# Where 1 / rms and the norm weight enter the two FFNs of a Hymba layer

## The chip, the cores and the metric

The kernel runs on one core of a Trainium2 chip. The time is the device time of one execution in microseconds; several executions give a median. The engines are TensorE (PE; PEld is its weight load), VectorE (DVE), ScalarE (ACT), GpSimd (POOL) and SyncE (SP), which issues most transfers.

## The reference, cut to what matters

One layer for a prompt of 1024 tokens with 16 meta tokens in front, and 8 sample tokens: T = 1048 tokens, D = 1024, D_FF = 2816, all fp32.

```python
def rmsnorm(x, w):
    y = xf * lax.rsqrt(jnp.mean(xf * xf, axis=-1, keepdims=True) + EPS)
    return (y * w.astype(jnp.float32)).astype(x.dtype)

def swiglu(x, wg, wu, wd):
    return (jax.nn.silu(x @ wg) * (x @ wu)) @ wd

# h += 0.5 * swiglu_1(rmsnorm(h));  h += mixers(rmsnorm(h)) @ w_out
# h += 0.5 * swiglu_2(rmsnorm(h));  final rmsnorm
```

The change concerns only `rmsnorm(h) @ wg` and `rmsnorm(h) @ wu`. Since 1 / rms is one factor per token and the norm weight one factor per input row, `rmsnorm(h) @ W = (1 / rms) * (h @ (w * W))`.

## The kernel before, in words

Activations are held transposed, features on the 128 partitions and tokens along the free axis. The tokens fall into two halves (c = 0, 1) of two quarters each, Q = 262 tokens a quarter. A product of fp32 accuracy is made of three matmuls (`mm3`, lines L143, L144 and L145): each operand is split into a high part (a ScalarE cast) and a low part (a VectorE subtraction). For weights these are L137 and L138, for activation operands L272 and L277.

**Gate and up by seven products.** FFN1 and FFN2 have 22 pairs each. A `pair` makes one block of 128 columns of gate and up for all tokens. Gate and up (two columns), the two halves of D (two rows) and the two quarters of a token half form a 2 x 2 by 2 x 2 block product, done with seven products instead of eight, in the order `ORDER = (1, 6, 2, 5, 7, 3, 4)`. Each product is done for both token halves, so a pair has 14 steps of 12 matmuls of 128x262. The left factors are sums of the four loaded weight tiles (gate and up, upper and lower rows; loads L354 numbered 1, 7, 4, 2; sums 5, 6, 7, 3 at L359), made anew for each pair. The right factors are sums of operand blocks (`Blocks`, sums L260), made once for each FFN and used by all 22 pairs.

**After a product** `post` works on it. Products 2, 3 and 4 accumulate in the banks of 1, 5 and 7:

| product | what post does |
|---|---|
| 1 | z: copy of the bank (ACT, L444) |
| 6 | v = bank + z (DVE, L446) |
| 2 | g0 = silu(bank) (ACT, L448) |
| 5 | x = bank + v (DVE, L450) |
| 7 | u1 = bank + x (DVE, L452) |
| 3 | g1 = silu(bank + v) (DVE L454, ACT L455) |
| 4 | u0 = bank + v (DVE, L457), then the hidden rows g * u (DVE, L462 twice) |

An accumulating product can start only when the post of the bank's first product has read it: 2 after z, 3 after x, 4 after u1.

**What sets the order.** Each FFN runs under a schedule written by hand (`manual_schedule` for PE, DVE, ACT and SP): a list of steps, and functions hung before a step with `S.before`. For a pair that begins at step s0, `LEADS` puts the four weight loads before steps s0 - 10, -10, -9, -9, the sums before -7, -7, -6, -5, and the seven splits before s0 - 4 + 2i. An engine works its queue in order. The hidden rows and differences of them (L534) are stored to DRAM by SP (L537) for the down projection, and the loads of the next pair's weights stand behind such stores in SP's queue.

**Operands before the change.** For FFN1, `Input` loads x in nine tiles of 128 tokens, squares them (L837), transposes them on PE, copies them to feature-major form, forms 1 / rms, spreads it over the partitions by a matmul with ones (L881), and multiplies it and the norm weight into the operand blocks (L890, 32 operations of 128x262). For FFN2, `Norm` sums the squares of h while `out_proj` still runs (L201, L202, `nf2.end`), forms 1 / rms (L159 to L163), and `Blocks.scaled` multiplies it and the norm weight into the blocks (L253, 32 operations). The first half's blocks are made in the second half of `out_proj`, the second half's after `out_proj`.

**Pools.** Operand blocks come from 30 `u` slots of T elements, hidden rows from 8 `s` slots, raw weights from 8, split weights from 6; PSUM has two 2-bank `acc` tiles and four `mis` banks.

Of the kernel before, what the change touches and what calls it, by code (L numbers as in the profile page):

```python
# [17 lines left out]
P = 128  # L18
# [163 lines left out]
class Norm:  # L182


    def __init__(self, K, h):
        self.K, self.h = K, h
        self.rt = {}
        self.sq = {}

    def r(self, q):  # L190
        return self.rt[q // 2][:, (q % 2) * Q : (q % 2) * Q + Q]
# [12 lines left out]
    def end(self, q, table=True):  # L204
        K = self.K
        if q // 2 not in self.rt:
            self.rt[q // 2] = K.t(2 * Q)
        ps = K.psm()
        K.nc.tensor.matmul(ps[:, :Q], K.ones[D], self.sq[q], start=True, stop=True)
        K.rstd(self.r(q), ps[:, :Q], Q, self.an if table else None)  # L210

# [29 lines left out]
class Blocks:  # L241


    def __init__(self, K, half):
        self.K, self.half = K, half
        self.b, self.op = {}, {}

    def scaled(self, norm, wcol):
        for p, k0, n in ((1, 0, 0), (7, 0, 1), (2, 4, 0), (3, 4, 1)):
            q = 2 * self.half + n  # L250
            self.b[p] = self.K.slot("u", T)
            for k in range(4):
                self.K.nc.vector.scalar_tensor_tensor(self.b[p][:, k * Q : k * Q + Q], norm.h[k0 + k][:, q * Q : q * Q + Q], wcol[:, k0 + k : k0 + k + 1], norm.r(q), ALU.mult, ALU.mult)  # L253

    def sum_(self, p):
        K, b = self.K, self.b
        x, y = {5: (7, 1), 6: (3, 5), 7: (3, 7), 4: (2, 6)}[p]
        if p not in b:
            b[p] = K.slot("u", T)
        K.nc.vector.tensor_sub(b[p], b[x], b[y])  # L260

    def sums(self):
        for p in (5, 6, 7, 4):
            self.sum_(p)

    def steps(self):


        def cast(*ps):
            for p in ps:  # L270
                self.op[p] = self.K.slot("u", T, F32R), self.K.slot("u", T, F32R)
                self.K.nc.scalar.copy(self.op[p][0], self.b[p])  # L272

        def low(*ps):
            for p in ps:
                hi, lo = self.op[p]
                self.K.nc.vector.tensor_sub(lo, self.b[p], hi.bitcast(F32))  # L277

        def begin():
            cast(1, 2)  # L280
            low(1)
            self.sum_(5)
            self.sum_(6)
            cast(6, 5)

        def more():
            low(5)
            self.sum_(7)
            cast(7, 3)

        def last():
            self.sum_(4)
            cast(4)
            low(7)

        return [begin, lambda: low(6), lambda: low(2), more, last, lambda: low(3, 4)]

    def split(self, p):
        K = self.K
        self.op[p] = K.slot("u", T, F32R), K.slot("u", T, F32R)  # L300
        K.split(self.b[p], *self.op[p])
# [44 lines left out]
def left(K, S, s0, srcs, n, at):  # L346


    nc = K.nc
    raw, w = {}, {}  # L350

    def load(p, src):
        raw[p] = K.raw(n * P)
        nc.sync.dma_start(raw[p].rearrange("p (k c) -> p k c", k=n), src)  # L354

    def sum_(p, x, y, op):
        if p not in raw:
            raw[p] = K.raw(n * P)
        nc.vector.tensor_tensor(raw[p], raw[x], raw[y], op)  # L359

    def split(p):
        w[p] = K.split_w(raw[p])

    loads = [lambda p=p, src=src: load(p, src) for p, src in zip((1, 7, 4, 2), srcs)]
    sums = [
        lambda: sum_(5, 7, 4, ALU.add),
        lambda: sum_(6, 5, 1, ALU.subtract),
        lambda: sum_(7, 1, 7, ALU.subtract),
        lambda: sum_(3, 2, 6, ALU.subtract),
    ]  # L370
    splits = [lambda p=p: split(p) for p in ORDER]
    if at:
        for fns, ds in zip((loads, sums, splits), at):
            for fn, d in zip(fns, ds):
                S.before(s0 + d, fn)
        return w
    return w, loads, sums, splits


LEADS = (-10, -10, -9, -9), (-7, -7, -6, -5), [2 * i - 4 for i in range(7)]  # L380
# [45 lines left out]
def pair(K, S, wg, wu, f, ops, hid, first=None):  # L426
# [8 lines left out]
    srcs = [wg[:, 0:4, fs], wu[:, 0:4, fs], wu[:, 4:8, fs], wg[:, 4:8, fs]]  # L435

    def temp(n, cs):
        if n not in tm:
            tm[n] = halves(K.t(2 * Q))
        return tm[n][:, cs]  # L440

    def post(p, cs, b):
# [4 lines left out]
        elif p == 2:  # L447
            nc.scalar.activation(temp("g0", cs), b, AF.Silu)  # L448
        elif p == 5:
            nc.vector.tensor_add(temp("x", cs), b, temp("v", cs))  # L450
        elif p == 7:
            nc.vector.tensor_add(temp("u1", cs), b, temp("x", cs))  # L452
        elif p == 3:
            nc.vector.tensor_add(temp("g1", cs), b, temp("v", cs))  # L454
            nc.scalar.activation(temp("g1", cs), temp("g1", cs), AF.Silu)  # L455
        else:
            nc.vector.tensor_add(temp("u0", cs), b, temp("v", cs))  # L457
            if "h" not in tm:
# [5 lines left out]
    if not first:  # L464
        w = left(K, S, s0, srcs, 4, LEADS if f > 1 else (*LEADS[:2], [2 * i - 3 for i in range(7)]))
        Unit(K, w, [o.op for o in ops], 4, post).both(S)
        return
    w, loads, sums, splits = left(K, S, s0, srcs, 4, None)
    order, blocks, between = first
    steps = [o.steps() for o in ops]  # L470
    if order == "w":
        between(loads, sums)
        blocks(0)
        splits[0]()
        for i, fn in enumerate(steps[0][:3]):
            fn()
            if i == 0:
                blocks(2)
            if i < 2:
                splits[i + 1]()  # L480
        for i, fn in enumerate(steps[0][3:]):
            S.before(s0 + 1 + i, fn)
            S.before(s0 + 1 + i, splits[3 + i])
        S.before(s0 + 1, lambda: blocks(3))
    else:
        for fn in loads:
            fn()
        blocks(0)
        for fn in steps[0] + sums + splits[:6]:
            fn()  # L490
        S.before(s0 + 6, between)
    S.before(s0 + 4, lambda: blocks(1))
    for i, fn in zip((4, 5, 5, 6, 7, 8), steps[1]):
        S.before(s0 + i, fn)
    S.before(s0 + 9, splits[6])
    unit = Unit(K, w, [o.op for o in ops], 4, post)
    for ps_ in (ORDER[:6], ORDER[6:]):
# [179 lines left out]
def ffn(K, wg, wu, wd, ops, src, first, after):  # L677
# [9 lines left out]
    with K.tc.manual_schedule(engines={E.PE, E.DVE, E.Activation, E.SP}):  # L687
        S = Steps()
        hidden = Hidden(K)
        for i in range(NF // 2):  # L690
            hid, e = [], []
            for f in (2 * i, 2 * i + 1):
                hid.append([])
                pair(K, S, wgv, wuv, f, ops, hid[-1], first if f == 0 else None)
# [98 lines left out]
def token_rows(i, meta, prompt, sample):  # L793

    if i == 0:
        return [(0, NM, meta), (NM, P - NM, prompt[0 : P - NM, :])] if meta is not None else [(NM, P - NM, prompt[0 : P - NM, :])]
    t0 = P * i - NM
# [5 lines left out]
class Input:  # L803
# [3 lines left out]
    def __init__(self, K, a, wcol, ops):  # L807
        self.K, self.wcol, self.ops = K, wcol, ops
        self.a = a
        self.b, self.x, self.n, self.r = {}, {}, {}, {}  # L810
        self.st = K.sml.tile([P, 3, 9], F32, tag="st0", name="st0", bufs=1)
# [874 lines left out]
```

## Time and profile before

| what | value |
|---|---|
| three runs | 2152.72, 2160.46, 2165.0 us; median 2160.46 |
| profiled execution | 2155.25 us, span 2153.5 us, mean granted clock 0.971 |
| busy share of the span | PE 94%, DVE 65%, ACT 36%, POOL 6% |
| FFN1: first product's matmul | 34.07 us |
| FFN1: second pair; end of the last pair | 87.20 us; about 517 us |
| FFN2: first product's matmul; second pair | 1412.49 us; 1456.1 us |
| FFN2: end of the last pair | about 1886 us |

A pair of steady state takes 20.46 us, and TensorE has no gap in it: 14 steps of 12 matmuls, 0.1218 us apart. A duration in a row of the trace is that of one operation; two operations of ScalarE or VectorE in a row overlap by some 0.1 us, so their starts lie closer than their durations (a cast of 128x512 lasts 0.61 us, and the next one starts after 0.51).

### The profile page before, as it was taken

To read this page: it belongs to the slowest core of one execution; us is meant where nothing else is said; L and a number is where in the kernel's file an instruction comes from. 1 tells how busy PE (TensorE), PEld (TensorE's weight loads), DVE (VectorE), ACT (ScalarE), POOL (GpSimd) and SP (SyncE) were. 2 spreads that over 40 slices of the span, in tenths; PEclk is the share of its full clock that TensorE was granted. 3 is DMA by queue.
4 is the path that set the end of the run, shared out by engine and by line. 5 is a ranking of instruction groups with operands and counts; after the bars stand their busy time and mean duration, and the time that the engine had idled before them with its cause. 6 is when DMAs were issued, how large, how long until landed. Compare 5 with 4: busy or idle time off the path is not lost.

```text
span 2153.5 us, 38152 instructions
## 1 busy us (share of the span) xinstructions
PE 2013.7 (94%) x15502; PEld 1960.3 (91%) x15502; DVE 1407.0 (65%) x2380; ACT 774.7 (36%) x1406; POOL 138.1 (6%) x175
## 2 busy tenths in 40 slices
PE   5799999999899899799999998969999999989996
PEld 4799999999899889688989987959999999989996
DVE  5766666666787675596365456776666666668863
ACT  5322222223334543572432335442222222324441
POOL 1000000000002110321011001210000000000000
PEclk6899999999999999899999999989999999999998
DMA  6142332337956511452022043213233242587741
GB/s 201 30 120 84 96 112 82 104 99 218 310 182 195 157 49 31 118 154 74 32 73 77 25 152 125 88 55 105 75 120 97 83 119 85 174 264 228 213 149 58
DMA packets 325031, 259.16 MB, mean 120 GB/s; under 512 B 17712, under 2 KB 301104, under 8 KB 324848
## 3 DMA queue, kind: packets, MB, share of 16 engines
q1 hardware_dynamic: 324040, 254.58, 39.3%
q8 instruction: 122, 2.00, 0.4%
q10 hardware_dynamic: 592, 2.10, 0.3%
q14 instruction: 53, 0.43, 0.1%
q0 software_dynamic: 224, 0.04, 0.0%
HBM read 191.26 MB, written 65.47 MB: 119 GB/s over the span
## 4 chain that ended last, share of the span: by engine, by line
PE 79%; DVE 10%; DMA 4%; ACT 3%; issue 2%; POOL 1%; SPq 0%; DVEq 0%; ACTq 0%; POOLq 0%
PE acc L143 24%; PE acc L144 24%; PE acc L145 24%; PE mis L1336 1%; DMA r<-in_w_ffn_down_dram 1%; DVE u L277 1%; DVE s L633 1%; DVE u L260 1%; DMA s<-in_x_prompt_dram 1%; DMA u<-hd 1%; DVE ws L138 1%; DVE s L1350 1%; DVE ws L615 1%; DVE s L1338 0%; PE mis L1375 0%
## 5 line engine op out<-in xcount | busy, mean ns | idle before, releaser
L143 PE MATMUL acc<-u,ws 128*128 128x262 f32 (+2 forms) x4504 | 1324.2, 295 | 72.1 <-DVE s L633 21.5
L144 PE MATMUL acc<-u,ws 128*128 128x262 f32 (+2 forms) x4504 | 1316.0, 292 | 6.2 <-DVE u L277 5.0
L145 PE MATMUL acc<-u,ws 128*128 128x262 f32 (+2 forms) x4504 | 1313.1, 292 | 0.1
L143 PEld LDWEIGHTS acc<-u,ws 128*128 128x128 f32 x4504 | 856.9, 190 | 90.6 <-issue 27.7
L144 PEld LDWEIGHTS acc<-u,ws 128*128 128x128 f32 x4504 | 860.6, 191 | 8.8 <-DVE u L277 5.9
L145 PEld LDWEIGHTS acc<-u,ws 128*128 128x128 f32 x4504 | 856.8, 190 | 0.9 <-DVE ws L615 0.6
L138 DVE TENSOR_TENSOR ws<-r,ws 128x512 fp32r<-128x512 f32 x396 | 272.7, 692 | 231.0 <-ACT ws L137 231.0
L137 ACT CAST ws<-r 128x512 fp32r<-128x512 f32 x396 | 227.0, 617 | 77.4 <-PE acc L145 58.2
L455 ACT ACTIVATE t<-t 128x524 f32<-128x524 f32 (+1 forms) x46 | 28.7, 623 | 314.3 <-DVE t L454 314.3
L359 DVE TENSOR_TENSOR r<-r,r 128x512 f32<-128x512 f32 x176 | 118.6, 693 | 13.4 <-DMA r<-in_w_ffn_up_dram 11.8
L202 POOL TENSOR_TENSOR t<-t,t 128x262 f32<-128x262 f32 x56 | 53.1, 964 | 815.9 <-ACT t L201 815.9
L633 DVE SCALAR_TENSOR_TENSOR s<-acc,s 128x524 f32<-128x524 f32 (+1 forms) x120 | 77.4, 661 | 41.5 <-PE acc L145 40.5
L562 DVE TENSOR_TENSOR u<-u,u 128x1048 fp32r<-128x1048 f32 (+1 forms) x84 | 96.9, 1158 | 8.4 <-ACT u L558 8.4
L448 ACT ACTIVATE t<-acc 128x524 f32<-128x524 f32 (+1 forms) x46 | 27.1, 589 | 182.2 <-PE acc L145 182.2
L610 ACT CAST ws<-r 128x512 fp32r<-128x512 f32 (+1 forms) x84 | 48.0, 582 | 104.1 <-DMA r<-in_w_ffn_down_dram 45.9
L558 ACT CAST u<-u 128x1048 fp32r<-128x1048 f32 (+1 forms) x84 | 83.2, 993 | 1.4 <-DMA u<-hd 1.4
L615 DVE TENSOR_TENSOR ws<-r,ws 128x512 fp32r<-128x512 f32 (+1 forms) x84 | 56.9, 690 | 40.5 <-ACT ws L610 40.5
L610 ACT CAST ws<-u 128x512 fp32r<-128x512 f32 (+1 forms) x72 | 42.1, 584 | 113.5 <-DVE u L605 110.0
L444 ACT COPY t<-acc 128x524 f32<-128x524 f32 (+1 forms) x46 | 26.5, 577 | 146.6 <-PE acc L145 146.6
L454 DVE TENSOR_TENSOR t<-acc,t 128x524 f32<-128x524 f32 (+1 forms) x46 | 31.2, 679 | 58.8 <-PE acc L145 58.8
L615 DVE TENSOR_TENSOR ws<-u,ws 128x512 fp32r<-128x512 f32 (+1 forms) x72 | 47.2, 656 | 28.4 <-ACT ws L610 28.4
L462 DVE TENSOR_TENSOR s<-t,t 128x524 f32<-128x524 f32 (+1 forms) x92 | 58.5, 677 | 1.6
(353 smaller groups left out, 1764.1 us busy)
## 6 DMA issues: line engine op xcount, KB each, us to landing
hd<-s SPq DMA_DIRECT2D x170, 262.0 KB
r<-in_w_ffn_down_dram SPq DMA_DIRECT2D x128, 256.0 KB
u<-hd SPq DMA_DIRECT2D x56, 524.0 KB
r<-in_w_ffn_gate_dram SPq DMA_DIRECT2D x88, 256.0 KB
r<-in_w_ffn_up_dram SPq DMA_DIRECT2D x88, 256.0 KB
r<-in_w_in_dram SPq DMA_DIRECT2D x56, 256.0 KB
r<-in_w_ffn_down_dram SPq DMA_DIRECT2D x64, 192.0 KB
u<-hd SPq DMA_DIRECT2D x28, 393.0 KB
```

Source lines behind the costliest of these rows:

```text
L137: self.nc.scalar.copy(hi, src)
L138: self.nc.vector.tensor_sub(lo, src, hi.bitcast(F32))
L143: mm(ps, whi, xhi, start=first, stop=False, skip_group_check=more)
L144: mm(ps, whi, xlo, start=False, stop=False, skip_group_check=more)
L145: mm(ps, wlo, xhi, start=False, stop=last, skip_group_check=more)
L359: nc.vector.tensor_tensor(raw[p], raw[x], raw[y], op)
L462: nc.vector.tensor_mul(halves(hid[0][:, n * 2 * Q : n * 2 * Q + 2 * Q])[:, cs], temp(f"g{n}", cs), temp(f"u{n}", cs))
L558: K.nc.scalar.copy(hi, lo.bitcast(F32))
L562: K.nc.vector.tensor_sub(lo, lo.bitcast(F32), hi.bitcast(F32))
L610: nc.scalar.copy(w[p, j, g][:, : n * P], src)
L615: nc.vector.tensor_sub(t[:, 512 : 512 + n * P], box[0], t[:, : n * P].bitcast(F32))
L633: nc.vector.scalar_tensor_tensor(t, b, 0.5, t, ALU.mult, ALU.add)
```

## The change

**FFN1 and FFN2, gate and up.** 1 / rms is no longer part of the operand blocks. It lies in one more `u` tile of the token length (`Spread`), held for the whole of gate and up, and `post` multiplies it in: four VectorE multiplications per pair, in g0 (which VectorE now reads from PSUM, and ScalarE's silu then takes in place), u1, g1 and u0.

```diff
+    def times_r(n, i, cs, src=None):
+        t = temp(n, cs)
+        nc.vector.tensor_mul(t, t if src is None else src, spread.lanes(i, cs))
+        return t
...
         elif p == 2:
-            nc.scalar.activation(temp("g0", cs), b, AF.Silu)
+            t = times_r("g0", 0, cs, b)
+            nc.scalar.activation(t, t, AF.Silu)
...
         elif p == 7:
             nc.vector.tensor_add(temp("u1", cs), b, temp("x", cs))
+            times_r("u1", 1, cs)
         elif p == 3:
             nc.vector.tensor_add(temp("g1", cs), b, temp("v", cs))
-            nc.scalar.activation(temp("g1", cs), temp("g1", cs), AF.Silu)
+            t = times_r("g1", 1, cs)
+            nc.scalar.activation(t, t, AF.Silu)
         else:
             nc.vector.tensor_add(temp("u0", cs), b, temp("v", cs))
+            times_r("u0", 0, cs)
```

**FFN1's norm weight** goes onto the weight rows. Each of a pair's four loaded tiles is scaled in place by ScalarE, four operations of 128x128 a tile, between load and sum. The loads stand one step earlier in the schedule. The class `Left` takes the place of the function `left`.

```diff
-LEADS = (-10, -10, -9, -9), (-7, -7, -6, -5), [2 * i - 4 for i in range(7)]
+class Left:
...
+    def scale(self, p):
+        if self.wcol is not None:
+            for k in range(self.n):
+                c = k + (self.n if p in (4, 2) else 0)
+                t = self.raw[p][:, k * P : k * P + P]
+                self.K.nc.scalar.activation(t, t, AF.Identity, scale=self.wcol[:, c : c + 1])
...
+    def plan(self, S, s0, late):
+        for ps, ds, fn in (
+            ((1, 7, 4, 2), (-11, -11, -10, -10), self.load),
+            ((7, 4, 1, 2), (-9, -8, -8, -7), self.scale),
+            ((5, 6, 7, 3), (-7, -7, -6, -5), self.sum_),
+            (ORDER, [2 * i - 4 + late for i in range(7)], self.split),
+        ):
```

**FFN2's norm weight** stays in the operand blocks and is multiplied in by ScalarE, without 1 / rms.

```diff
-                self.K.nc.vector.scalar_tensor_tensor(self.b[p][:, k * Q : k * Q + Q], norm.h[k0 + k][:, q * Q : q * Q + Q], wcol[:, k0 + k : k0 + k + 1], norm.r(q), ALU.mult, ALU.mult)
+                self.K.nc.scalar.activation(t[:, k * Q : k * Q + Q], h[k0 + k][:, q * Q : q * Q + Q], AF.Identity, scale=wcol[:, k0 + k : k0 + k + 1])
```

**FFN2's start** (`first2`; o and e are the first and the second half's blocks). The second half's blocks are begun in front of the first product, by the schedule's order before the 1 / rms of that half (`nf2.end(2)`, `nf2.end(3)`), which moves before the third step. The first pair's products come in the order 1, 5, 2, 6, 7, 3, 4. The rows of h that down needs (`keep2(1)`) are stored from step 6.

```diff
+        e.scaled(h, wn2, (1, 7))
+        e.cast(1)
+        e.sum_(5)
+        e.low(1)
+        e.cast(5)
+        e.low(5)
+        e.scaled(h, wn2, (2, 3))
...
+        before(1, (e.cast, 2), (e.sum_, 6), (e.low, 2))
+        before(2, (e.cast, 6), (e.sum_, 7), (nf2.end, 2), (nf2.end, 3, False), (e.low, 6))
+        before(3, (e.cast, 7), (e.sum_, 4), (e.low, 7))
+        before(4, (e.cast, 3), (e.low, 3))
+        before(5, (e.cast, 4), (e.low, 4))
+        before(6, (keep2, 1))
+        before(8, (w.split, 4))
+        return 1, 5, 2, 6, 7, 3, 4
```

**FFN1's start** (`first1`). x is cut into ten tiles that end at the token half, all loaded by SP, transposed and copied straight into the operand blocks as it is. The squares, 1 / rms (`x.rms`) and its spreading (`x.spread_r`, a matmul with ones and ScalarE copies) move into the steps of the first pair, whose products come in the order 1, 2, 5, 6, 7, 3, 4. In both first pairs `post_first` runs the post of 5 after that of 6, and that of 2 after u1.

```diff
+        before(3, (w.sum_, 7), (w.hi, 7), (o.low, 7), (w.lo, 7), (x.rms, 0), (o.cast, 3), (x.place, 7, act))
+        before(4, (x.spread_r, 0), (w.sum_, 3), (w.hi, 3), (o.low, 3), (w.lo, 3), (o.sum_, 4), (o.cast, 4), (x.place, 8, act), (x.place, 9, act), (x.store, 1))
...
+        before(8, (x.rms, 1), (w.split, 4), (e.low, 7), (e.sum_, 4), (e.cast, 3))
+        before(9, (e.low, 3), (e.cast, 4))
+        before(10, (x.spread_r, 1), (e.low, 4))
+        return 1, 2, 5, 6, 7, 3, 4
```

## The prediction, written before the changed kernel was run

> **What bounds the kernel now.** I read the page first (busy times, then the chain), then windows of single pairs, then the timeline of one pair by engine, last the waits of TensorE.
>
> ```profile
> PE 2013.7 (94%) x15502; PEld 1960.3 (91%) x15502; DVE 1407.0 (65%) x2380; ACT 774.7 (36%) x1406; POOL 138.1 (6%) x175
> PE 79%; DVE 10%; DMA 4%; ACT 3%; issue 2%; POOL 1%; SPq 0%; DVEq 0%; ACTq 0%; POOLq 0%
> ```
>
> TensorE sets the time; VectorE and ScalarE matter where a stage starts, and wherever they become late inside a pair. Windows of three neighbouring pairs of FFN1 (after the window and its length: PE, PEld, DVE, ACT, POOL busy, clock, DMA share, GB/s):
>
> ```profile
> 250.97:271.43 20.46, 20.46 (x170) 20.46 (x169) 12.33 (x19) 5.46 (x10) 0.00 (x0) 1.00 0.27 78
> 271.43:292.27 20.84, 20.68 (x170) 20.50 (x169) 13.55 (x21) 5.46 (x10) 0.00 (x0) 1.00 0.39 115
> 292.27:312.73 20.46, 20.46 (x170) 20.46 (x169) 12.33 (x19) 5.46 (x10) 0.00 (x0) 1.00 0.28 79
> ```
>
> A pair takes 20.46 us and leaves VectorE 8.1 us idle. The middle one took 20.84. Why, its timeline on VectorE and on SP shows, and TensorE's waits in 271 to 292.4:
>
> ```profile
> 271.54 0.70 DVE L457 TENSOR_TENSOR t<-acc,t 128x524 f32<-128x524 f32 x1 [0.33 <-PE acc L145]
> 272.27 1.32 DVE L462 TENSOR_TENSOR s<-t,t 128x524 f32<-128x524 f32 x2
> ...
> 284.07 1.42 DVE L359 TENSOR_TENSOR r<-r,r 128x512 f32<-128x512 f32 x2 [1.92 <-DMA r<-in_w_ffn_up_dram]
> 285.40 0.69 DVE L450 TENSOR_TENSOR t<-acc,t 128x524 f32<-128x524 f32 x1
> ```
> ```profile
> 273.62 1.86 SPq L537 DMA_DIRECT2D hd<-s  x3
> 275.57 0.57 SPq L354 DMA_DIRECT2D r<-in_w_ffn_gate_dram  x1
> 276.24 0.51 SPq L354 DMA_DIRECT2D r<-in_w_ffn_up_dram  x1
> 276.94 0.52 SPq L537 DMA_DIRECT2D hd<-s  x1
> 277.56 0.56 SPq L354 DMA_DIRECT2D r<-in_w_ffn_up_dram  x1
> ```
> ```profile
> PE acc L143 <- DVE t L450: 0.2, 1, 0.2
> ```
>
> This is the line to learn from. The sum L450 (x) empties the bank into which product 3 accumulates. On VectorE it stands behind two weight sums for the next pair (L359), and these wait for weights that SP loads only after the hidden rows have been stored. Here the weights came late, x ended 14.56 us after the pair's first L457 began, and the pair grew by 0.38. So x has to end 14.18 us after L457; the other FFN1 pairs end it between 12.3 and 13.8. The margin is 0.4 to 1.9 us.
>
> **Steady FFN1 pairs: the term that decides.** Four multiplications of 128x524 are added per pair, 44 pairs: four by 0.62 (start to start) is 2.5 us of VectorE, within the 8.1 idle, so free by themselves. But one stands between L457 and the hidden products, so the stores, and the loads queued on SP behind them, go 0.72 later (L457 to L462 is 0.73).
>
> In FFN1 each loaded weight tile also gets 4 ScalarE scalings of 128x128 before VectorE may sum it. Four cost 1.18, and 1.09 until the next starts:
>
> ```profile
> 39.72 1.18 ACT L872 ACTIVATE t<-ident,st 128x128 f32<-128x128 f32 x4
> 40.81 1.12 ACT L137 CAST ws<-r 128x512 fp32r<-128x512 f32 x2
> ```
>
> ScalarE is in order, and its order in the changed kernel is: scale tile 7 (the second load), silu g0, one weight half, scale tile 4, scale tile 1, scale tile 2. The second weight sum waits for tile 1. From the second landing: 0.05 + 1.09 + 0.55 (silu of 0.64, overlapped) + 0.51 (cast of 0.61, overlapped) + 2.27 (eight scalings) = 4.47; then 0.08 to VectorE, and 1.31 from the second L359's start to x's end (284.79 to 286.10 above). So x ends 5.86 after the second load lands, and that must be by 14.18 - 5.86 = 8.32. In before's landing records (from L457) the second load lands at 8.2, 8.3, 8.6 and 8.9 in pairs with two stores ahead of it, and at 9.0, 9.2, 9.3 and 9.9 with three. With 0.72 added the means are 9.2 and 10.1: stalls of 0.9 and 1.75 at product 3, 1.3 per pair. Pairs 2 to 21 load and scale for a successor: 20 x 1.3 = **+26 us**. The end below is 0.3 a pair (loads land as early as now, since a store no longer stands between the second and third): +6; above 2.3: +46.
>
> The Trainium skill (ScalarE: Activation LUTs, What ACT_TABLE_LOAD costs) gives 186 ns + 0.833 ns per element, 93 ns more per pointer operand and 93 ns of overlap: 293 ns for each 128x128 scaling in a row where the trace has 0.27. By its figure twelve scalings take 0.3 longer and this term would be some 6 us larger; the row decides.
>
> **FFN2 pairs** scale nothing. Their latest x ends at 14.38 already; 0.72 more stalls one or two pairs: +1 (0 to +4).
>
> **FFN1's start.** Removed: 32 multiplications L890, 2 x 6.4 us of VectorE, both in the chain, and the wait for 1/rms ahead of the first product (34.07). Waits of TensorE from 20 to 88:
>
> ```profile
> PE acc L143 <- DVE t L454: 12.2, 1, 12.2
> PE acc L881 <- ACT t L872: 8.7, 1, 8.7
> ```
>
> Now the transposes still wait for the small parameters (landed 10.5), end at 15.4; copies 0.7, cast 1.07, weight half 0.6: first product at about 17, 17 us sooner. What comes next is ScalarE's queue, from 12.9 on: ten squares 10.6, fourteen casts of 0.97, ten weight halves of 0.51, eight tiles to scale 8.7, place copies 6.3, three table loads 3.8, diagonals 2.7, small ones 3.5: 54 us, where before's ScalarE was busy 41 in all up to 87. Without idling it ends at 67. But each cast of a sum waits for VectorE (1.25 there, 1.07 back), and the second 1/rms waits for the last square behind casts and scalings; walking the queues with these durations puts the second half's 1/rms at 79.4 and the second pair at 86.7, against 87.20. I take **-0.5** (-13 if ScalarE never idles, +8 if each handover costs as much as before).
>
> **out_proj and FFN2's start.** Between 1370 and 1410 VectorE was busy 4.2 to 5.0 of each 5 us and TensorE had gaps of 0.4 to 1.4, 6.8 in all. Sixteen L253 (6.4 us) go from VectorE to ScalarE as 16 x 0.42: **-2** (-5 to +2). At FFN2's start before:
>
> ```profile
> PE acc L143 <- ACT t L444: 8.2, 1, 8.2
> PE acc L143 <- ACT u L272: 5.5, 1, 5.5
> ```
>
> From its first matmul (1412.49) to the second pair 43.6 us pass, 23 more than a full pair. Sixteen more L253 leave (6.4), a table load too (1.28), and the second half is begun earlier. But its scalings now stand on ScalarE ahead of the copy z of the first product: after the last weight half (0.86) nine ops of 0.42, cast 1.0, cast of sum 5 until 6.9, eight ops more until 10.2, then z until 10.6. Product 2 accumulates in z's bank and waits for it: it starts at 10.6 where 2.9 was possible. x of the first half stands on VectorE behind 1/rms (ScalarE 12.6 to 16.2 with its table, VectorE until 18) and three block operations of 1.2: 22.2, and product 3 waits for it. Then z of the second half (29.7) and its 1/rms products (38); second pair at about 42.5: **-1** (-10 if z slips in early, +6).
>
> **Pair to down.** A tile for 1/rms holds one of 30 operand slots; down's first loads of hidden rows then find one free, not two, where DMA share is 0.96 to 1.01: **+1.5** per FFN, +3 (0 to +6).
>
> Sum: +26 + 1 - 0.5 - 2 - 1 + 3 = +26.5 on the profiled execution's 2155.25 (span 2153.5): 2182. The median of three stands 5.2 above that execution; I give 2184, between.
>
> **Rivals.**
> - *x stays on time, and the starts pay: faster.* Decided by the second landing: up to 8.3 us after L457 there is no stall. For it: two landings of 8.2 and 8.3. Against: the loads are issued later, not earlier. With no stall, -13 at FFN1's start, -2, -1, +3: about 2143.
> - *Nearly no stall, and no start gain: no change.* 0.3 a pair (+6), -0.5, -2, -1, +3: about 2161.
> - *The clock falls with the stall.* A gap of 2.76 before 728.06 was followed by matmuls 0.12 apart at clock 1.00; after 3.55 (2118.62) fifteen ran 0.22 apart: 1.5 us lost. If stalls pass some 3 us in each pair: at least 20 x (3 - 1.3 + 1.5) = 64 more, 2246; in the pairs with three stores alone, 2214. Against it: my largest stall is 2.3. The Trainium skill (TensorE: Matmul & The Clock Gate, HAM oscillation — how this bites in real kernels) describes just this for waits over about 3.4 us repeated every tile; the two gaps of the trace lie on either side of that.
> - *FFN2's second half does not begin early in effect*, since z waits: that is in the forecast (-1), not the 10 to 15 which the moved work suggests.
>
> **Chances.** Forecast 0.61 (slower), clock 0.08 (slower), nearly no stall 0.17 (no change), starts pay 0.14 (faster). 0.5%, 10.8 us, is about what a measurement can tell from no change. Range: the forecast with its bounds 2160 to 2206; to hold 8 in 10 it reaches toward 2143 and 2214: 2148 to 2212.
>
> **What would show it.** Right: FFN1 pairs of 21.3 and 22.2 us in turn, with TensorE waiting for x (the sum in p5's post) before product 3, and VectorE's second weight sum waiting for a ScalarE scaling; first product near 17, second pair near 87; in FFN2's start a wait for the copy z of some 7 us. FFN2's pairs still 20.46. Wrong: FFN1 pairs of 20.46 (the landing or ScalarE's order misjudged), or a second pair before 80.

## The result, and the profile after

| | before | after |
|---|---|---|
| median of four runs each | 2159.48 us (2152.72 to 2165.0) | 2224.68 us (2221.64 to 2226.61) |
| profiled execution, span | 2155.25, 2153.5 us | 2225.85, 2224.1 us |
| mean granted clock | 0.971 | 0.965 |

The changed kernel is slower: ratio 1.0302, 95% interval 1.027 to 1.0335. The direction was forecast; the size, 65 us, is more than twice the 24 to 26 forecast, and the time lies 13 us above the range.

The page of the changed kernel, busy times and then the chain that ended last:

```profile
PE 2044.1 (92%) x15494; PEld 1983.2 (89%) x15494; DVE 1495.2 (67%) x2498; ACT 894.5 (40%) x1799; POOL 141.9 (6%) x175
PE 58%; DVE 16%; DMA 9%; ACT 7%; issue 4%; SPq 1%; POOL 1%; DVEq 0%; ACTq 0%; POOLq 0%
```

Every other engine still has more than 30% to spare. What changed is the chain: TensorE carries 58% of it where it carried 79%, and VectorE, transfers and ScalarE carry the rest. So the loss has to be looked for in the order of the queues. Three neighbouring FFN1 pairs as windows, from one L475 (u0) to the next (length, then busy time of PE, PEld, DVE, ACT, POOL, clock, DMA share, GB/s):

```profile
206.90:229.13 22.23, 19.58 (x149) 19.40 (x148) 14.47 (x24) 10.16 (x26) 0.00 (x0) 0.92 0.38 109
229.13:251.65 22.52, 21.47 (x176) 21.29 (x176) 14.97 (x24) 10.18 (x26) 0.00 (x0) 1.00 0.24 71
251.65:274.50 22.85, 20.15 (x166) 19.97 (x165) 15.59 (x26) 9.77 (x26) 0.00 (x0) 1.00 0.39 106
```

A pair took 20.46 us before; over pairs 2 to 21 it now takes 23.65 in the mean. The middle window on VectorE:

```profile
229.13 0.70 DVE L475 TENSOR_TENSOR t<-acc,t 128x524 f32<-128x524 f32 x1
229.86 0.70 DVE L454 TENSOR_TENSOR t<-t,u 128x524 f32<-128x524 f32 x1
230.60 1.32 DVE L481 TENSOR_TENSOR s<-t,t 128x524 f32<-128x524 f32 x2
...
240.59 0.69 DVE L376 TENSOR_TENSOR ws<-r,ws 128x512 fp32r<-128x512 f32 x1 [2.35 <-ACT ws L372]
241.78 0.69 DVE L368 TENSOR_TENSOR r<-r,r 128x512 f32<-128x512 f32 x1 [0.49 <-ACT r L362]
242.95 0.69 DVE L368 TENSOR_TENSOR r<-r,r 128x512 f32<-128x512 f32 x1 [0.48 <-ACT r L362]
243.56 0.69 DVE L466 TENSOR_TENSOR t<-acc,t 128x524 f32<-128x524 f32 x1
...
249.12 0.70 DVE L454 TENSOR_TENSOR t<-t,u 128x524 f32<-128x524 f32 x1
251.04 0.69 DVE L376 TENSOR_TENSOR ws<-r,ws 128x512 fp32r<-128x512 f32 x1 [1.22 <-ACT ws L372]
251.65 0.70 DVE L475 TENSOR_TENSOR t<-acc,t 128x524 f32<-128x524 f32 x1
```

and on ScalarE and SP:

```profile
238.24 1.28 ACT L362 ACTIVATE r<-r,col 128x128 f32<-128x128 f32 x4 [4.88 <-DMA r<-in_w_ffn_up_dram]
239.43 0.62 ACT L464 ACTIVATE t<-t 128x524 f32<-128x524 f32 x1
239.96 0.60 ACT L372 CAST ws<-r 128x512 fp32r<-128x512 f32 x1
240.46 3.62 ACT L362 ACTIVATE r<-r,col 128x128 f32<-128x128 f32 x12
...
249.86 0.64 ACT L473 ACTIVATE t<-t 128x524 f32<-128x524 f32 x1 [4.74 <-DVE t L454]
250.41 1.12 ACT L372 CAST ws<-r 128x512 fp32r<-128x512 f32 x2
```
```profile
231.33 2.34 SPq L545 DMA_DIRECT2D hd<-s  x2
233.77 0.56 SPq L355 DMA_DIRECT2D r<-in_w_ffn_gate_dram  x1
234.42 1.05 SPq L355 DMA_DIRECT2D r<-in_w_ffn_up_dram  x2
```

Read them as one loop. SP stores hidden rows as soon as L481 has made them, then issues the loads. ScalarE waits 4.88 us for the second load, and everything behind it in its queue waits too: silu g0, the rounding of product 3's weights (L372 at 239.96), twelve more scalings. VectorE waits 2.35 us for that rounding (L376 at 240.59), then twice for scaled tiles, and only then empties the bank for product 3 (x, L466, ending at 244.25, 15.12 after L475). At the other end u0 (L475 at 251.65) stands behind an L376 that waits 1.22 us for a rounding that stands behind silu g1. u0 makes the next hidden rows, and the loop starts again. All of TensorE's waits from 88 to 562:

```profile
PE acc L143 <- DVE t L466: 44.3, 20, 4.0
```

Twenty waits for x, 2.2 us each. TensorE lost more than these 44.3 us: in 7 of the 20 pairs such a wait was followed by 13 to 26 matmuls some 0.22 us apart in place of 0.12, about 14 us in all. The offset of the changed kernel's profile against the one before, landmark by landmark, adds up to the 70.6 us between the spans:

| stretch | forecast | measured |
|---|---|---|
| up to the first FFN1 pair's last u0 (the second pair's start) | -0.5 | +1.1 |
| FFN1 pairs 2 to 21 | +26 | +63.7 (409.3 to 473.0) |
| last FFN1 pair; FFN1's down | +1.5 | +1.1; +2.9 |
| mixers; out_proj | none; -2 | -3.0; +0.9 |
| FFN2's start, to the first pair's last u0 | -1 | -2.2 |
| FFN2's pairs 2 to 21 | +1 | +1.8 |
| last FFN2 pair; FFN2's down; end | +1.5 | +2.0; +2.1; +0.4 |

### The profile page after: what moved, and what is told of

It reads as the page before. It is cut to its first block, busy times and chain, and to the rows that moved or that the text cites. A ratio compares the mean times of both kernels' runs of the same rounds, so it can differ in the third digit from the quotient of the medians.

```text
span 2224.1 us, 38759 instructions
## 1 busy us (share of the span) xinstructions
PE 2044.1 (92%) x15494; PEld 1983.2 (89%) x15494; DVE 1495.2 (67%) x2498; ACT 894.5 (40%) x1799; POOL 141.9 (6%) x175
## 4 chain that ended last, share of the span: by engine, by line
PE 58%; DVE 16%; DMA 9%; ACT 7%; issue 4%; SPq 1%; POOL 1%; DVEq 0%; ACTq 0%; POOLq 0%
PE acc L143 18%; PE acc L144 17%; PE acc L145 17%; DMA r<-in_w_ffn_up_dram 5%; ACT r L362 4%; DVE t L454 2%; DVE ws L376 2%; DMA r<-in_w_ffn_down_dram 2%; PE mis L1328 1%; ACT ws L372 1%; DVE s L481 1%; DVE r L368 1%; DMA u<-hd 1%; DVE s L641 1%; DVE s L542 1%
## 5 line engine op out<-in xcount | busy, mean ns | idle before, releaser
L143 PEld LDWEIGHTS acc<-u,ws 128*128 128x128 f32 x4504 | 867.5, 193 | 139.5 <-ACT r L362 46.0
L144 PEld LDWEIGHTS acc<-u,ws 128*128 128x128 f32 x4504 | 872.0, 194 | 4.6 <-DVE u L299 1.9
L145 PEld LDWEIGHTS acc<-u,ws 128*128 128x128 f32 x4504 | 868.6, 193 | 2.9 <-DVE ws L376 2.2
L376 DVE TENSOR_TENSOR ws<-r,ws 128x512 fp32r<-128x512 f32 x308 | 212.2, 689 | 162.9 <-ACT ws L372 162.9
L372 ACT CAST ws<-r 128x512 fp32r<-128x512 f32 x308 | 175.0, 613 | 5.9 <-PE acc L145 5.1
L362 ACT ACTIVATE r<-r,col 128x128 f32<-128x128 f32 x352 | 108.0, 388 | 119.5 <-DMA r<-in_w_ffn_up_dram 119.5
L473 ACT ACTIVATE t<-t 128x524 f32<-128x524 f32 (+1 forms) x46 | 28.7, 623 | 269.2 <-DVE t L454 269.2
L454 DVE TENSOR_TENSOR t<-t,u 128x524 f32<-128x524 f32 (+1 forms) x138 | 93.9, 680 | 4.6
L464 ACT ACTIVATE t<-t 128x524 f32<-128x524 f32 (+1 forms) x46 | 28.3, 616 | 119.2 <-DVE t L454 119.2
```

The source lines that it names most:

```text
L143: mm(ps, whi, xhi, start=first, stop=False, skip_group_check=more)
L144: mm(ps, whi, xlo, start=False, stop=False, skip_group_check=more)
L145: mm(ps, wlo, xhi, start=False, stop=last, skip_group_check=more)
L362: self.K.nc.scalar.activation(t, t, AF.Identity, scale=self.wcol[:, c : c + 1])
L372: self.K.nc.scalar.copy(self.w[p][:, : self.n * P], self.raw[p])
L376: self.K.nc.vector.tensor_sub(t[:, 512 : 512 + w], self.raw[p], t[:, :w].bitcast(F32))
```

## The experiments

The theory: the four multiplications by 1 / rms are hidden, and the sixteen scalings on ScalarE turn the order of the queues inside a pair into a loop that is longer than TensorE's 20.46 us. Rivals: VectorE's extra work is itself the loss; or the clock is; or the first pairs are. Where only the step numbers of `Left.plan` are edited, the diff shows the lines of the plan. Where no ratio is given, the time is that of a single run; the 45 runs of the kernel before lie between 2149.91 and 2165.0 us.

**No scaling** (e1). The kernel leaves FFN1's norm weight out.

```diff
-        if self.wcol is not None:
+        if False:
             for k in range(self.n):
```


> FFN1's weight rows are not scaled (the norm weight of FFN1 is left out of the computation); all else as in the changed kernel, whose FFN1 pairs take 23.6 us on average. Theory A (a loop without TensorE sets the pair: hidden product L481, store, load, ScalarE scaling, weight sum, x, u1, g1, then ScalarE's hi of product 6, VectorE's lo, u0, hidden product): without the 4.5 us of ScalarE between landing and sum, x ends about 12.5 to 14 us after L475, TensorE no longer waits, pairs of 20.46 to 20.7, total about 2224 - 60 = 2164. Theory B (the four multiplications on VectorE make the pair long, the scaling only adds x's lateness of 1.7): pairs of about 22, total about 2190. Theory C (DMA lands later than before for another reason): no change, 2224.

2161.16 us, beside 2159.51 for the kernel before. Pairs take 20.5 us with all four multiplications in place, and VectorE as busy as in the changed kernel. TensorE's waits from 82 to 500:

```profile
PE acc L143 <- DVE t L466: 1.0, 2, 0.7
```

So the multiplications are hidden, and the scalings, where they stand, are what costs. The first pair's last u0 also comes at 82.81, 5.9 us sooner than in the changed kernel.

**The weight sums later** (e2).

```diff
-            ((5, 6, 7, 3), (-7, -7, -6, -5), self.sum_),
+            ((5, 6, 7, 3), (-4, -4, -4, -3), self.sum_),
```


> The weight sums go behind x and u1 on VectorE (offsets -4, -4, -4, -3 in place of -7, -7, -6, -5), nothing is left out. Theory A: x no longer waits for the landing, and TensorE goes on to product 3 at once; the loop has 8 us of slack, pairs of 20.46 to 20.6, total about 2164. Theory B (VectorE's added work): pairs stay above 22, total above 2190. Rival inside A: the weights' split for the next product 1 or 6 comes late instead, pairs of 21 to 22 with the wait moved to products 1 or 6, total 2175 to 2195.

2253.26 us, worse, with pairs of 24.6. Some of the waits from 88 to 560:

```profile
DVE ws L376 <- ACT ws L372: 161.8, 57, 6.9
ACT r L362 <- DMA r<-in_w_ffn_up_dram: 141.3, 19, 9.2
...
PE acc L143 <- DVE t L471: 23.6, 18, 1.4
PE acc L143 <- DVE t L466: 19.8, 18, 3.2
```

x is no longer behind the sums, but still behind L376 of product 3, whose rounding waits on ScalarE behind a scaling that waits for the load. And the sums now stand ahead of g1 and u0, so the stores and the next loads come later still. A step moved out of the way on one engine is paid for on another.

**The loads earlier** (e3).

```diff
-            ((1, 7, 4, 2), (-11, -11, -10, -10), self.load),
+            ((1, 7, 4, 2), (-13, -13, -12, -12), self.load),
```


> The weight loads are issued two steps earlier (offsets -13, -13, -12, -12), so the first two stand on SP ahead of the hidden rows' stores; order on VectorE and ScalarE as in the changed kernel. Theory A: the second load lands about 3 us earlier, x ends at 12.3 to 13.3 after L475, pairs of 20.46 to 20.6, total about 2164. If ScalarE's order (scale 7, silu g0, hi, scale 4, scale 1) is the bound whatever the landing, x still waits for silu g0 behind product 2 and ends at about 14.5: pairs of 21, total about 2175. Theory B: above 2190.

2187.37 us: 37 of the 65 come back. From the third on, pairs alternate between 20.6 us (x ends 13.2 after u0) and 21.4 to 22.2 (14.0 to 14.8), and pairs 2 to 21 take 426.3 us, 17 more than before the change; eleven waits of ScalarE for a load are left (44.5 us from 88 to 500), and eleven of TensorE for x (12.9 us from 88 to 560). The landing is a part of the loop, not all of it.

**The split of product 6 after u0** (e4), which takes away the 1.22 us in front of u0; the edit moves nothing else.

```diff
-            (ORDER, [2 * i - 4 + late for i in range(7)], self.split),
+            (ORDER, [0 if i == 1 else 2 * i - 4 + late for i in range(7)], self.split),
```


> Only product 6's weight split (hi on ScalarE, lo on VectorE) goes from two steps ahead of the next pair to its first step, so u0 (L475) no longer stands behind a lo that waits for a hi behind silu g1. Theory A: from x's end to the next L475 takes 6.3 us where it takes 7.4 now; 20 pairs x 1.1 = 22 less, x still ends 1.7 late and TensorE still waits for it: total about 2200. If only x's lateness counts and u0's place does not: no change, 2224. It may instead stall product 6 (lo late by up to 1 us): then 2215 to 2225.

2211.75 us. FFN1's pairs 2 to 21 took 449.0 us in place of 473.0. From x's end to the next u0 it took 6.27 us in 19 of the 20 pairs, where the changed kernel takes 7.40, so u0's place in VectorE's queue was worth some 22 us there. x still ended late, 16.1 after u0 (15.8 in the changed kernel, 5 us in all the other way), and half clock followed the wait in one pair in place of seven (some 7 us less). TensorE's waits from 88 to 560 begin with:

```profile
PE acc L143 <- DVE t L466: 22.5, 20, 2.5
PE acc L145 <- DVE ws L376: 6.3, 20, 0.3
```

FFN2's pairs, where the same numbers hold, lost about 11 us, of which 5.8 were waits of TensorE for the split itself, 0.3 in each pair; that is about what separates the total from the 2200 expected.

**Scalings and sums one step later, the split of product 6 one step earlier** (e5).

```diff
-            ((7, 4, 1, 2), (-9, -8, -8, -7), self.scale),
-            ((5, 6, 7, 3), (-7, -7, -6, -5), self.sum_),
-            (ORDER, [2 * i - 4 + late for i in range(7)], self.split),
+            ((7, 4, 1, 2), (-8, -7, -7, -6), self.scale),
+            ((5, 6, 7, 3), (-6, -6, -5, -4), self.sum_),
+            (ORDER, [-3 if i == 1 else 2 * i - 4 + late for i in range(7)], self.split),
```


> Only the order in FFN1 and FFN2 pairs is changed, nothing is left out: scalings one step later (-8, -7, -7, -6), so that on ScalarE silu g0 and product 3's hi stand ahead of the first scaling, which waits for the landing; sums at -6, -6, -5, -4, so that x stands ahead of them on VectorE; product 6's split one step earlier (-3), so that its hi stands ahead of silu g1. Theory A (the landing reaches TensorE through the in-order queues of ScalarE and VectorE, in the run with later sums through product 3's hi behind scaling 7): no wait for x is left, pairs of 20.46 to 20.7, total 2160 to 2170. Theory A' (the chain landing, three scalings, two sums is too long for a pair wherever it stands): the wait shows at u1 or at the next product 1, pairs of 21 to 22, total 2175 to 2195.

2185.1 us, pairs of 21.5. x now ends 12.15 after u0 and is never waited for. VectorE in one pair:

```profile
252.85 0.70 DVE L466 TENSOR_TENSOR t<-acc,t 128x524 f32<-128x524 f32 x1 [0.31 <-PE acc L145]
255.88 0.69 DVE L376 TENSOR_TENSOR ws<-r,ws 128x512 fp32r<-128x512 f32 x1 [2.33 <-ACT ws L372]
256.49 2.01 DVE L368 TENSOR_TENSOR r<-r,r 128x512 f32<-128x512 f32 x3
258.42 0.70 DVE L468 TENSOR_TENSOR t<-acc,t 128x524 f32<-128x524 f32 x1
```

The wait has moved on by one bank: u1 (L468) stands behind three sums, these behind an L376 that waits 2.33 us for a rounding that stands behind twelve scalings. TensorE waits for u1 in each pair (13.5 us in 19 waits from 88 to 500).

**FFN2's first pair reordered** (e6): most of the work on the second half's blocks stands behind the first half's z, v or x instead of ahead.

```diff
         e.cast(1)
-        e.sum_(5)
-        e.low(1)
-        e.cast(5)
-        e.low(5)
-        e.scaled(h, wn2, (2, 3))
...
+        before(1, (e.sum_, 5), (e.low, 1), (e.scaled, h, wn2, (2, 3)), (e.cast, 5))
+        before(4, (e.low, 5), (e.cast, 2), (e.sum_, 6))
```


> Only FFN2's first pair is reordered: the second half's scalings for products 2 and 3 and its casts go behind the first half's z, v and x, and 1/rms of the second half to step 7; FFN1 pairs stay at 23.6. If z's and x's places in the queues cause FFN2's long start (42 us from its first matmul to the second pair's first L475, waits for z, x and z again), the second pair starts 7 to 12 us sooner: total 2224 - 10 = 2214, and the wait for the first z is gone. If ScalarE's work as such bounds the start, it gains 0 to 3.

2223.44 us. From out_proj's last sum to the first pair's last u0 it takes 39.0 us in place of 42.2: less than half of the 7 to 12 us that were expected if z and x were the bound, and about what the other case gave (0 to 3). TensorE's two largest waits in this stretch, in the changed kernel and then in this one:

```profile
PE acc L143 <- ACT t L459: 6.9, 2, 5.1
PE acc L143 <- DVE t L466: 5.4, 1, 5.4
```
```profile
PE acc L143 <- DVE t L454: 8.0, 2, 6.6
PE acc L143 <- ACT t L459: 3.9, 2, 2.5
```

12.3 us of waits became 11.9: z and x came earlier, and a product with 1 / rms (L454) was late in their place. Some 14 fewer matmuls at half clock account for 1.4 of the 3.1 us gained.

**Both, and FFN1's first pair reordered too** (e7): e5 and e6, the last five squares of FFN1's second half behind the splits and five copies of `x.place` on VectorE, the second pair's scalings and sums another step later.

```diff
-        before(5, (e.cast, 1), (e.low, 1), (e.cast, 2), (e.sum_, 5), (e.low, 2), (e.cast, 5), (x.square, 5))
+        before(5, (e.cast, 1), (e.low, 1), (e.cast, 2), (e.sum_, 5), (e.low, 2), (e.cast, 5))
...
-        before(7, (e.low, 6), (e.sum_, 7), (e.cast, 7), (x.square, 8), (x.square, 9))
+        before(7, (e.low, 6), (e.sum_, 7), (e.cast, 7), *((x.square, i) for i in range(5, 10)))
```


> The two reorderings together, and in FFN1's start the second half's squares behind its last cast, the placing copies of tiles 5 to 9 on VectorE, the second pair's scalings and sums one step later. By theory A: FFN1 pairs 20.46 to 20.7 (-60), FFN2's start -10, FFN1's start -3 to -8 (the second half's z no longer behind squares and scalings): 2224 - 75 = 2149, about 0.5% under the kernel before. By theory A' (chain too long): 2165 to 2185.

2183.35 us, ratio 1.0111 (1.0076 to 1.0146). FFN2's start takes 36.7 us, but FFN1's pairs still take 21.5 as in e5, and that is what stays. The time lies where the expectation put a chain too long for a pair (A'); e8 shows that it was not too long.

**u1 freed, in two ways** (e8, e9), both on e7.

```diff
e8:
-            ((7, 4, 1, 2), (-8 + late, -7 + late, -7 + late, -6 + late), self.scale),
+            ((7, 4, 1, 2), (-8 + late, -7 + late, -6 + late, -6 + late), self.scale),
e9:
-            ((5, 6, 7, 3), (-6 + late, -6 + late, -5 + late, -4 + late), self.sum_),
+            ((5, 6, 7, 3), (-6 + late, -4 + late, -4 + late, -4 + late), self.sum_),
```


> As the version with all reorderings (e7), with one more edit: the four scalings of block 1 one step later on ScalarE, behind the rounding of product 4's weights. In e7 the three weight sums stood ahead of u1 on VectorE because lo of product 4 (L376) waited 2.3 us for its hi, which stood behind twelve scalings (3.62 us); u1 came 0.9 us late in each pair, and pairs took 21.5 us. Theory (a pair's time is set by the order of VectorE's and ScalarE's queues alone): lo of product 4 comes 1.2 us earlier, the three sums with it, u1 is no longer waited for, pairs take 20.4 to 20.6 us; 21 pairs x 1.0 = 21 less, so 2160 to 2166 us, the time before within 0.5%. Rival (the loads behind the hidden stores are the true bound, 21 us or more a pair): u1 is early but the scalings wait for the landing, PE waits for x again; pairs 21 to 22, 2172 to 2190.

> As e7, with the weight sums of products 6, 7 and 3 behind u1 on VectorE instead (sum 5 alone stays ahead of it); scalings as in e7. Theory: u1 stands behind lo of product 4 and one sum, and ends about when TensorE needs it (product 4 waits at most 0.2); g1 and u0 come about 1 us later than in e7 relative to TensorE, so the hidden stores and the loads behind them do too; pairs 20.5 to 20.8, 2161 to 2169 us. Rival (the loop over stores and loads has no slack): the later u0 comes back as a wait of the scalings for the landing and of product 7 for x; pairs 21 to 22, 2172 to 2190. If e8 and e9 differ, the slack lies in the load loop and not in VectorE.

e8: 2163.12 us, ratio 1.002 (1.0003 to 1.0037). Pairs take 20.44 us. VectorE, then ScalarE, of one of them:

```profile
264.67 0.70 DVE L466 TENSOR_TENSOR t<-acc,t 128x524 f32<-128x524 f32 x1 [0.32 <-PE acc L145]
266.53 0.69 DVE L376 TENSOR_TENSOR ws<-r,ws 128x512 fp32r<-128x512 f32 x1 [1.15 <-ACT ws L372]
267.14 2.07 DVE L368 TENSOR_TENSOR r<-r,r 128x512 f32<-128x512 f32 x3
269.12 0.69 DVE L468 TENSOR_TENSOR t<-acc,t 128x524 f32<-128x524 f32 x1
```
```profile
263.54 2.45 ACT L362 ACTIVATE r<-r,col 128x128 f32<-128x128 f32 x8
265.89 0.60 ACT L372 CAST ws<-r 128x512 fp32r<-128x512 f32 x1
266.40 2.45 ACT L362 ACTIVATE r<-r,col 128x128 f32<-128x128 f32 x8
```

All sixteen scalings are still there; eight stand ahead of the rounding and eight behind it, VectorE waits 1.15 in place of 2.33, and u1 starts 4.45 us after x started, 5.57 in e5. e9 took 2177.4 us (ratio 1.0095, 1.0073 to 1.0116), more than its theory gave: pairs of 21.4. u1 was on time, but g1 (L471) now stood behind the sums:

```profile
PE acc L143 <- DVE t L471: 17.1, 19, 1.2
```

ScalarE did not wait for loads there (4.6 us in all from 88 to 530), so this is again VectorE's order, not the rival's loop over stores and loads, to which the expectation would have put a difference between e8 and e9. The wait for g1 is at the next pair's product 1, which takes the `acc` tile that product 3 has left; the expectation took g1 to have room.

**The remains, and a version beside the kernel before** (e10, e11; twelve runs each).

```diff
e10, on e8:
-            ((7, 4, 1, 2), (-8 + late, -7 + late, -6 + late, -6 + late), self.scale),
+            ((7, 4, 1, 2), (-8 + late, -7 + late, -6, -6 + late), self.scale),
-            at = [b + k for k in (-14, -11, -11, -9, -9, -7)], [b + k for k in (-8, -7, -6, -5, -4, -2)]
+            at = [b + k for k in (-14, -11, -11, -9, -9, -7)], [b + k for k in (-8, -7, -5, -4, -3, -2)]
e11, on e10:
-        for at, p in ((e0 + 2, 1), (e1 + 1, 3), (e1 + 2, 2)):
+        for at, p in ((e0 + 2, 1), (e1 + 1 + (i == FP - 1), 3), (e1 + 2, 2)):
```


> As e8, with two small edits for what was still slower than before there: the second pair's scaling of block 1 back where e7 had it (its two first periods were 2.1 us longer in e8), and in the last pair of each FFN the rounding of four of the six first operands of the down product one step later, since two of them stood ahead of u1 on VectorE (TensorE waited 1.19 and 0.89 us there, 0.43 in the kernel before). Theory: 2 less in FFN1's start, 1 to 1.5 less in each FFN's last pair; 2157 to 2161 us, no difference from the kernel before that can be measured, or up to 0.1% less. Rival: the operands' second parts, which now stand ahead of g1 and u0 instead, are late for the down product's first steps, and give back what u1 gains; 2160 to 2164.

> As e10, and in the last pair one store of the hidden block (the one for product 3) one step later on SP, behind the loads of down weights that follow it; in e8 ScalarE waited 8.3 us for those weights and TensorE 3.2 us for the accumulator that VectorE freed late behind them (1.1 in the kernel before). Theory: SP no longer waits 12 to 13 us for this store with the load behind it, the weights land 5 us or more earlier, the wait of 3.2 us in each FFN goes; 2152 to 2157, faster than the kernel before by 0.1 to 0.3%. Rival: another store, one step on, holds the same queue, or the buffers set when the weights are loaded: as e10.

e10: 2156.28 us against 2158.94, ratio 0.9987 (0.9977 to 0.9997), the first version below the kernel before, by 0.1%. The last pair takes 24.71 us in place of e8's 25.60 in FFN1 (23.55 before the change) and 24.96 in place of 25.84 in FFN2 (23.54). e11: 2157.05 us, ratio 0.999 (0.9978 to 1.0002): in the same stretch from 500 to 560 TensorE's wait for the accumulator fell from

```profile
PE acc L143 <- DVE s L641: 2.3, 1, 2.3
```

to

```profile
PE acc L143 <- DVE s L641: 0.6, 1, 0.6
```

but from the last u0 to the end of FFN1's down it took 247.3 us in both. One wait went, and 14 matmuls at half clock after a later gap of 2.67 us are 1.4 us the other way; e10 has the same gap, and no half clock behind it. The gain that was expected did not come; the rival's "as e10" did.

**Nine numbers alone** (e12): the changed kernel, both first pairs as the change has them.

```diff
-            ((7, 4, 1, 2), (-9, -8, -8, -7), self.scale),
-            ((5, 6, 7, 3), (-7, -7, -6, -5), self.sum_),
-            (ORDER, [2 * i - 4 + late for i in range(7)], self.split),
+            ((7, 4, 1, 2), (-8, -7, -6, -6), self.scale),
+            ((5, 6, 7, 3), (-6, -6, -5, -4), self.sum_),
+            (ORDER, [-3 if i == 1 else 2 * i - 4 + late for i in range(7)], self.split),
```


> The changed kernel with nothing but nine step numbers of the pairs' weight plan altered as in e8 (scalings one step later, block 1's two; weight sums one step later; rounding of product 6 one step earlier), both FFNs' first pairs as the change has them. Theory (the order of the queues within the pairs is the whole of the loss beyond the starts): 20 FFN1 pairs at 20.45 in place of 23.65, 64 us less than the changed kernel: 2158 to 2166. Rival (part of the loss comes from FFN1's start, which the other versions altered too): 2170 or more.

2162.75 us in the one run, 62 less than the changed kernel's median. TensorE's waits from 88 to 500, and two pairs as windows:

```profile
PE acc L143 <- DVE t L468: 0.5, 1, 0.5
PE acc L143 <- ACT ws L372: 0.3, 1, 0.3
```
```profile
231.00:251.41 20.41, 20.41 (x168) 20.28 (x168) 15.63 (x25) 10.29 (x26) 0.00 (x0) 1.00 0.41 118
251.00:271.44 20.44, 20.44 (x169) 20.26 (x168) 14.93 (x24) 10.19 (x26) 0.00 (x0) 1.00 0.28 79
```

Not one operation was taken away, VectorE and ScalarE are as busy in a pair as in the changed kernel, and pairs 2 to 21 take 412.0 us in place of 473.0. The order of the queues within the pairs is nearly the whole loss.

## Why the prediction was right and wrong

**Right.** The engine, the bank and the chain: VectorE's x late behind the second weight sum, this behind ScalarE's scalings, these behind a load behind a store. The second load landed as forecast: the first scaling starts 9.73 us after L475 in the mean, where 9.65 + 0.05 was forecast. The four multiplications are hidden (e1), and the stores do go later by one of them (L475 to L481 1.47 us in most pairs, where L457 to L462 was 0.73). The first product at 17.43 (17 forecast), the second half's 1 / rms spread by 80.2 (79.4 forecast), no gain at the second pair (+1.1 for -0.5). FFN2's start was -2.2 for -1, on the path that was forecast: product 2 waits 5.1 us for the first half's z (some 7 forecast), and the second half's z ends 28.0 us after the first matmul (29.7 forecast).

**Right by luck: out_proj.** The forecast was -2, and mixers and out_proj together measured -2.1. But out_proj itself, from its first sum (L1453, now L1445) to its last, takes 107.7 us in place of 106.8. In its second half VectorE was busy 41.0 us in place of 47.7, as forecast, and nothing was gained by it. The forecast had also read the trace too high: between 1370 and 1410 TensorE has five gaps of 0.4 to 1.2 us, 4.0 in all and not 6.8, and it waits 2.4 us of that for VectorE; VectorE was busy 3.5 to 5.0 of each 5 us. The 3.0 us came in the mixers ahead of it, which the change does not touch; why, no run shows.

**Wrong: the step "stalls of 0.9 and 1.75 at product 3, 1.3 per pair", and with it the term +26.** It measured +63.7, in three parts.

- *x itself.* It ends 15.84 after L475 in the mean, 1.66 past the 14.18 that TensorE allows: 20 x 1.66 = 33, where 26 was forecast. The price of a scaling was taken as 0.27 from a row of four; twelve in a row took 3.62, which is 0.293 from one to the next. Twelve lie between the load and x: 12 x 0.023 = 0.28 a pair. The rows bear most of it out: from the first scaling to x's end it takes 6.01 us in 18 of the 20 pairs, where 5.81 was forecast, which is 4 of the 7; two odd pairs (7.34 and 6.60) make 2 more. The Trainium skill (ScalarE: Activation LUTs, What ACT_TABLE_LOAD costs) has figures from which just that follows, an estimate of 293 ns for such an operation in a row; the prediction named it and went by the row.
- *The step that was missing: what L457 itself waits for.* The stall was counted from L457 to x, as if L457 (now L475) came when TensorE's product 4 ended. Before, it did, 0.04 behind. Now x's delay goes on through ScalarE (silu g1 behind g1 times 1 / rms, the rounding for product 6 behind silu g1) and holds up VectorE in front of u0. From x's end to the next L475 pass 7.40 us in 12 of the 13 pairs without half clock, where 20.46 - 14.18 = 6.28 would do: 20 x 1.12 = 22. e4 took away this wait, and there it took 6.27.
- *The clock.* It was a rival by itself at 0.08, and bound to stalls of over some 3 us. It came in beside the forecast's own mechanism: in 7 of 20 pairs TensorE ran 13 to 26 matmuls at half clock. In these seven the stretch from x's end to L475 is 8.06 to 9.04 us in place of 7.40, which makes the remaining 63.7 - 33 - 22 = 8 us. TensorE itself lost some 14 us by them, but a part of that lay behind the 1.12 us by which L475 was late anyway. No run removed the clock alone.

**Pair to down** (+3 forecast, 0 to 6). This term was wrong too: last pair and down together were 1.1 + 2.9 in FFN1 and 2.0 + 2.1 in FFN2, 8.1 in all. The forecast gave an operand slot as the reason. In the last pair it was in part VectorE's order: TensorE waits 0.9 us for u1 in the changed kernel, and e10, which frees u1 from two roundings of operands, took 0.9 us off e8's last pair in each FFN. The downs did not come back by it (FFN1's 247.3 us in e10, 247.1 in the changed kernel, 244.2 before). In them 18 and 25 more matmuls ran at half clock than before, 1.7 and 2.5 us; TensorE's gaps grew by some 2 us in FFN1's down and not in FFN2's. The slot was not tried, and the rest stays open.

**Rivals.** "Starts pay" and "nearly no stall" both fell with x: there was a wait in each of the 20 pairs. That the second landing decides was half right: with loads two steps earlier (e3) pairs 2 to 21 still lost 17 us, while with the loads as they were and another order (e12) next to nothing was waited for there (0.8 us).

## What to carry to other kernels

When an in-order engine gets new work, follow the queue both ways round: not only who waits for the new work, but whether that delay comes back to the start of the same period. A stall that is part of such a loop can be more than one lateness times the number of periods, since it may lengthen every link that it passes: here 63.7 us in all, of which the first link was 33. And before dropping a change for it, move the new operations by a step: eight scalings on each side of one rounding were worth 20 us more than twelve and four (e7 to e8).

## What the runs showed of the hardware

**A gap's length alone did not decide the clock.** A gap is taken here from the start of one matmul to the start of the next. In FFN1's pairs of the changed kernel gaps of 2.14, 2.31 and 2.93 us were followed by 13 to 16 matmuls some 0.22 us apart, and gaps of 3.22 to 4.31 by 23 to 26; gaps of 2.66, 2.72 and 2.98 were followed by none. In FFN1's down the same gap of 2.67 us was followed by 14 in e11 and by none in e10. The prediction took a limit between 2.76 and 3.55 from two gaps.

What decided, the traces show: how much of the gap fell into one step of a grid. In FFN1's pairs the granted clock changes only at times that lie whole multiples of 3.41 us apart (150.05, 153.47, 173.95, 177.36 and so on). On that grid, the steps around the gaps of 2.14 and of 2.98 us (after the window and its length: PE, PEld, DVE, ACT, POOL busy, clock, DMA share, GB/s):

```profile
146.64:150.05 3.41, 1.55 (x13) 1.37 (x12) 2.12 (x4) 3.41 (x12) 0.00 (x0) 1.00 0.00 0
150.05:153.47 3.42, 3.42 (x17) 3.42 (x17) 3.35 (x6) 0.53 (x2) 0.00 (x0) 0.50 0.03 7
...
262.69:266.11 3.42, 2.39 (x20) 2.17 (x18) 1.38 (x2) 3.42 (x11) 0.00 (x0) 1.00 0.37 116
266.11:269.52 3.41, 1.75 (x14) 1.78 (x15) 2.83 (x5) 2.38 (x7) 0.00 (x0) 1.00 0.00 0
269.52:272.93 3.41, 3.41 (x30) 3.41 (x29) 3.34 (x6) 0.00 (x0) 0.00 (x0) 1.00 0.00 0
```

The first gap left TensorE idle for 1.86 us of one step, and the next step ran at half clock; the second was split into 1.03 and 1.66, and cost nothing. Over FFN1's pairs (88 to 530 us) in all 14 traces, 19 steps with 1.86 us or more of idle time were each followed by a step at half clock, and 1770 steps with 1.77 or less by none. It also tells e11 from e10: the gap of 2.67 put 2.38 us into one step in e11, and at most 1.69 in e10. Elsewhere, in the mixers above all, half clock sometimes followed steps with less idle time, so this is a count from these pairs and not a full rule.

The Trainium skill (TensorE: Matmul & The Clock Gate, HAM oscillation — how this bites in real kernels) sets the limit at waits of over about 3.4 us; here 2.14 was enough. The Trainium skill (TensorE: Matmul & The Clock Gate, What's actually happening) also says that the window runs freely. The traces agree: steps of the grid began at 749.27 us in e10 and at 750.19 in e11, and so the outcome of a short gap can change from one to the next.
